# Three projection banks, one chain bank, later transposes and head sums, and weight parts kept in DRAM, in a hybrid decoder trunk

## The chip, the core and the metric

The kernel runs on one core of a Trainium2 chip. Its engines have queues of their own: TensorE (PE, with weight loads as PEld), VectorE (DVE), ScalarE (ACT), GpSimd (POOL) and SyncE (SP), which here only issues DMAs. The accumulator PSUM has eight banks of 128 x 512 float32 numbers. The metric is the device time of one execution in microseconds (us), as the median of several runs.

## What is computed

One layer of a decoder that mixes two kinds of heads, for a prompt of 2048 tokens and, beside it, for eight sequences of four new tokens each (32 sample tokens) with a state from before. The model is 1024 wide; all is float32. Cut to what matters, with the order of the kernel's tiles in mind:

```
h = rmsnorm(x, norm_w)
proj = h @ w_in                               # 1024 -> 3200 columns: 25 tiles of 128
p_rwkv, g_rwkv, u_pool, g_pool = split(proj, [1664, 2176, 2688])
ps = p_rwkv + mu_shift * (previous token's p_rwkv - p_rwkv)
r, k, v, xw, xa = split(ps)                   # 512, 512, 512, 64, 64
decay = exp(-exp(-softplus(-(w0 + tanh(xw) @ w_decay_b)) - 0.5))
a = sigmoid(a0 + xa @ w_aaa_b)
kk = k * k_k;  kk = kk / norm of kk per head;  k = k * (1 + (a - 1) * k_a)
for each token:                               # 8 heads of 64
    sa = S @ (-kk)
    S = S * decay + outer(sa, kk * a) + outer(v, k);  y = S @ r
y = group_norm(y) * gn_w + gn_b
o_rwkv = (y + sum(r * k * r_k) * v) * silu(g_rwkv)
o_pool = (windowed mean of u_pool - u_pool) @ pool_w * pool_scale * silu(g_pool)
out = rmsnorm(x + concat(o_rwkv, o_pool) @ w_out, norm_f)
```

The last rows of the shifted columns and of the pool's input and the last states S are outputs too.

## The kernel before

**Groups and tiles.** The prompt runs in `NG` = 4 groups of 512 tokens. Within a group the 25 column tiles of the projection follow in a fixed order (line 300): tile 12, which holds the two low-rank inputs, and then for each of four pairs of heads j six tiles: r, k, the pool's input, v, the pool's gate and the RWKV gate (`unit`). A projection (`proj`) multiplies a tile of the weights with eight slices `kc` of x. Both factors are split into two parts of the type fp32r, high and low, so there are three matmuls of 128 x 512 for each slice (lines 330 to 332: `xh,wh`, `xl,wh`, `xh,wl`), 24 to a tile, and they gather in one PSUM bank, `pp`. There are two such banks. The bank is read out behind the last matmul by ScalarE and VectorE (`shift`: `t1`, two steps, and `carry`, line 358; `lora_in`: `sa`, line 370; or `gate`). In the last group each tile has two halves of 272 columns, since the sample tokens ride along. The output projection (`out_tile`) comes behind the four groups and uses the same tag.

**The weights.** `w_load` brings a tile of the weights (512 KB, `wr`) by a DMA that ScalarE issues, two tiles ahead. `w_split` makes the parts one tile ahead, when the third slice's matmuls have been written: ScalarE copies `wh` (line 312), and VectorE subtracts to get `wl` (line 313). `wr`, `wh` and `wl` have two buffers each. All this is done anew in each of the four groups: 100 loads and 100 splits.

**The state's recurrence.** It runs for one pair at a time, in chunks of 64 tokens (`NCH` = 8 in a group). `key_norms` squares the keys, splits them (`head_sums`: `h_sq` on ScalarE, line 454, the rest on VectorE), lets `DH` = 6 steps go by and then sums over each head on TensorE (`sq`, line 461; a second such sum is `bo`). `products` makes the matrices within a chunk (`pa`, line 570, from `bk` and `abd`). `solve` has GpSimd solve triangular systems X (lines 636 and 638), which TensorE then transposes (`xt`, line 658). `fold` makes a matrix F for each chunk. `pair_chain` carries the state through the eight chunks: per step two matmuls `ch` (line 751) into one of two `ch` banks; VectorE makes the next state `SV` from partitions 64 to 127 of the bank (line 753), and ScalarE copies the outputs `Y` from partitions 0 to 63 (line 755). At the end `pair_back` norms Y on VectorE (its last step is line 778), waits one step and transposes it on TensorE (`try`, line 788, four matmuls).

**What sets the order.** Each of these is a generator. `proj` yields after each slice's three matmuls, and at each yield `side` lets every lane of the recurrence write its next piece. So a number of yields is a delay in slices of a projection, in the order in which the program is written. A scheduler of the compiler's framework then places the instructions on their engines by priority and by its own model of when each could run, so the order of the program is not kept everywhere. Each engine works through its list in order; an instruction that waits holds up all behind it.

**PSUM.** The eight banks are two each for `pp`, `ch`, `mm` (head sums, `xt`, products and others) and `pt` (`try` among them). The first two projections use the `ch` banks.

Of the kernel before, what the change touches and what calls it, by code (L numbers as in the profile page):

```python
# [9 lines left out]
F32 = mybir.dt.float32  # L10
F32R = mybir.dt.float32r
# [49 lines left out]
def tile_trunk(ctx, tc, xT, xtok, xsT, xstok, par, w_in, wlora, pool_w, w_out, norm_f, st_shift, st_wkv, st_pool,  # L61
# [239 lines left out]
    raws, wts, mark = {}, {}, {}  # L301

    def w_load(i):
        if i < len(order):
            raws[i] = sb.tile([P, KC, P], F32, tag="wr", name=f"wr_{i}")
            nc.scalar.dma_start(raws[i], w_in[order[i][1]])

    def w_split(i):
        if i < len(order):
            hi = sb.tile([P, KC, P], F32R, tag="wh", name=f"wh_{i}")  # L310
            lo = sb.tile([P, KC, P], F32R, tag="wl", name=f"wl_{i}")
            A.activation(hi, raws[i], AF.Copy)  # L312
            V.tensor_tensor(out=lo, in0=raws[i], in1=hi.bitcast(F32), op=sub)  # L313
            wts[i] = hi, lo
            del raws[i]

    def proj(g, m, xs):

        i = order.index((g, m))
        hi, lo = wts.pop(i)  # L320
        w_load(i + 2)
        last = g == NG - 1
        segs = []
        w = 272 if last else 512
        for s in range(2 if last else 1):
            pp = bank("pp" if i >= 2 else "ch", f"pp_{g}_{m}_{s}", 2)
            c = slice(s * w, (s + 1) * w)
            for kc in range(KC):
                xh, xl = xs[kc]
                PE.matmul(pp[:, :w], hi[:, kc, :], xh[:, c], start=(kc == 0), stop=False)  # L330
                PE.matmul(pp[:, :w], hi[:, kc, :], xl[:, c], start=False, stop=False)  # L331
                mark[0] = PE.matmul(pp[:, :w], lo[:, kc, :], xh[:, c], start=False, stop=(kc == KC - 1)).ins  # L332
                if s == 0 and kc == 2:
                    w_split(i + 1)
                if not last or kc % 2:
                    yield
            if g == 0 and m != 12:
                V.tensor_tensor(out=pp, in0=pp, in1=rb0[0], op=mult)
            if last:
                A.activation(spr[:, m, 16 * s:16 * s + 16], pp[:, 256:272], AF.Copy)  # L340
                segs.append((pp, 256 * s, 256))
            else:
                segs.append((pp, 0, G))
        return segs
# [55 lines left out]
    pend = [0]  # L400
    made = [None]
    lanes = {"prod": [], "solve": [], "fold": [], "chain": [], "x": [], "tail": []}
    late = []
# [80 lines left out]
    def key_norms(g, j, u, kk2, prod):  # L484

        nm = f"{g}_{j}"
        a = head_sums(kk2, f"sq_{nm}")
        for _ in range(DH):
            yield
# [220 lines left out]
    def fold(g, j, u):  # L710
# [27 lines left out]
        yield  # L738

    def pair_chain(g, j, u):  # L740
        nm = f"{g}_{j}"
# [3 lines left out]
        for cc in range(NCH):  # L745
            while u["folded"] <= cc:
                yield

            ch = bank("ch", f"ch_{nm}_{cc}", 2, (P, 2, 64))
            for h in range(2):  # L750
# [29 lines left out]
    def pair_back(g, j, u, Y):  # L780
        nm = f"{g}_{j}"
        yn = Y.rearrange("p a h v -> p (a h) v")
        group_norm(yn, yn, P, 8, nm)
        for _ in range(1):
            yield
# [82 lines left out]
    def sample(ret):  # L868
# [154 lines left out]
        for it in range(ST - 1):  # L1023
            yield
            x = bank("ch", f"s_it{it}", 2, (P, 8, 64))
            for hd in range(8):
                PE.matmul(x[0:NS, hd, :], Ab[:, hd, 0, :], sa[:, hd, :], start=True, stop=True)
            V.tensor_tensor(out=sa, in0=x[0:NS], in1=P0, op=add)
            V.tensor_tensor(out=sa, in0=sa, in1=d64, op=mult)
        yield  # L1030
        Y = bank("ch", "s_Y", 2, (P, 8, 64))
        for hd in range(8):
# [87 lines left out]
    def out_tile(o, res, dst, n, wo, nm):  # L1120
# [12 lines left out]
        for f in range(2):  # L1133
            pp = bank("pp", f"po_{nm}_{f}", 2)
            for c in range(8):
# [128 lines left out]
```

## Time and profile before

| | us |
|---|---|
| runs | 1295.18, 1299.73, 1302.32 |
| median | 1299.73 |
| the profiled execution | 1301.06 |
| its span in the trace | 1299.3 |

| engine | busy us | share of the span | instructions |
|---|---|---|---|
| TensorE, matmuls | 1195.8 | 92% | 7229 |
| TensorE, weight loads | 981.2 | 76% | 7229 |
| VectorE | 905.2 | 70% | 2103 |
| ScalarE | 633.3 | 49% | 1438 |
| GpSimd | 532.9 | 41% | 1138 |

HBM gave 100.07 MB and took 20.59 MB in this execution. The four groups lie at about 10 to 266, 266 to 530, 530 to 773 and 773 to 1040 us, the output from 1040 to the end.

How it is read: the span runs from the first to the last event of the trace. Busy times of matmuls and of weight loads overlap. A matmul's row gives its whole passage through the engine (0.39 us for 512 columns), while the next starts 0.23 us after it, so the distances of starts, and not the durations, tell the pace. The granted clock is the share of TensorE's full speed that the chip let it have; 1.00 stands for 2.4 GHz and 0.50 for 1.2 GHz. What stands behind `<-` at an idle time is the instruction that ended the wait, as the profile infers it.

### The profile page before, as it was taken

What the parts mean: (1) busy time and instruction counts of PE and PEld (TensorE: products, weight loads), DVE (VectorE), ACT (ScalarE), POOL (GpSimd) and SP (SyncE); (2) the same over time, 40 slices, a digit from 0 to 9 for tenths busy, and PEclk for the clock granted to TensorE, in tenths of its full rate; (3) what the DMA queues carried; (4) which work ended last, traced back from release to release, by engine and by line L of the source; (5) the groups of instructions that cost most, each with busy time, mean ns of one, the idle gap of its engine ahead of it and who ended that gap; (6) DMA issues with size and microseconds to landing.
All of it is one profiled execution on the core that took longest, in us unless ns stands there. A gap on an engine that the chain in (4) does not pass through costs nothing.

```text
span 1299.3 us, 21202 instructions
## 1 busy us (share of the span) xinstructions
PE 1195.8 (92%) x7229; PEld 981.2 (76%) x7229; DVE 905.2 (70%) x2103; ACT 633.3 (49%) x1438; POOL 532.9 (41%) x1138
## 2 busy tenths in 40 slices
PE   6997999969999898999999998989899999999997
PEld 3775777747777777777777787989898977887685
DVE  6765877776777667866777788666567667744765
ACT  3573545455655454656554557454545453321111
POOL 6064847360728171828083818273517280000000
PEclk7998999988999898999999999999899999998999
DMA  5352433232453332334443334322232444433332
GB/s 182 82 157 62 110 86 92 71 105 79 118 145 102 80 92 80 107 86 136 110 115 95 95 91 122 95 74 87 65 95 68 129 130 140 146 119 98 114 114 72
DMA packets 135371, 134.63 MB, mean 104 GB/s; under 512 B 80480, under 2 KB 97120, under 8 KB 135264
## 3 DMA queue, kind: packets, MB, share of 16 engines
q1 hardware_dynamic: 102432, 78.68, 21.2%
q10 hardware_dynamic: 32832, 54.60, 14.4%
q8 instruction: 57, 0.93, 0.3%
q14 instruction: 50, 0.41, 0.1%
HBM read 100.07 MB, written 20.59 MB: 93 GB/s over the span
## 4 chain that ended last, share of the span: by engine, by line
PE 47%; DVE 14%; ACT 5%; issue 3%; DMA 1%; ACTq 0%; DVEq 0%
PE pp L330 6%; PE pp L331 6%; PE pp L332 5%; PE po_o L1137 5%; PE po_o L1138 4%; PE po_o L1140 4%; PE f L723 3%; PE pa L570 2%; PE ch L751 2%; DVE wl L313 2%; DVE abd L518 1%; PE z L715 1%; PE pb L601 1%; PE q L685 1%; ACT rb L605 1%
## 5 line engine op out<-in xcount | busy, mean ns | idle before, releaser
L330 PE MATMUL pp<-xh,wh 128*128 128x512 f32 (+1 forms) x1000 | 378.7, 380 | 33.8 <-DVE carry L358 8.2
L331 PE MATMUL pp<-xl,wh 128*128 128x512 f32 (+1 forms) x1000 | 373.0, 373 | 5.0 <-DVE xl L256 2.6
L332 PE MATMUL pp<-xh,wl 128*128 128x512 f32 (+1 forms) x1000 | 369.1, 369 | 3.0 <-DVE wl L313 3.0
L330 PEld LDWEIGHTS pp<-xh,wh 128*128 128x128 f32 x1000 | 194.5, 195 | 64.2 <-ACT wh L312 14.7
L636 POOL TENSOR_TENSOR Xt<-X,L 128x60 f32<-128x60 f32 (+24 forms) x496 | 209.0, 421 | 38.9
L331 PEld LDWEIGHTS pp<-xl,wh 128*128 128x128 f32 x1000 | 194.7, 195 | 32.6 <-DVE xl L256 5.1
L332 PEld LDWEIGHTS pp<-xh,wl 128*128 128x128 f32 x1000 | 194.6, 195 | 28.6 <-DVE wl L313 6.2
L638 POOL TENSOR_TENSOR X<-X,Xt 128x60 f32<-128x60 f32 (+24 forms) x496 | 186.4, 376 | 38.9
L313 DVE TENSOR_TENSOR wl<-wr,wh 128x1024 fp32r<-128x1024 f32 x100 | 130.8, 1308 | 35.3 <-ACT wh L312 34.1
L631 POOL TENSOR_TENSOR X<-dmask,a 128x256 f32<-128x256 bf16 x16 | 12.6, 787 | 326.3 <-DVE a L628 326.3
L312 ACT ACTIVATE wh<-wr 128x1024 fp32r<-128x1024 f32 x100 | 105.5, 1055 | 58.1 <-PE pp L331 47.5
L751 PEld LDWEIGHTS ch<-SV,F 128*128 128x128 f32 x512 | 78.4, 191 | 13.4 <-DVE F L726 4.5
L751 PE MATMUL ch<-SV,F 128*128 128x64 f32 x512 | 79.3, 261 | 2.1 <-DVE F L726 1.2
L629 POOL TENSOR_TENSOR L<-L,a 128x1024 f32<-128x1024 f32 x16 | 30.6, 1914 | 123.3 <-DMA L<-dA 123.3
L723 PE MATMUL f<-zbd,ka 128*128 128x256 f32 x256 | 68.4, 388 | 3.5 <-DVE zbd L718 2.1
L1137 PE MATMUL po_o<-woh,oh_o 128*128 128x512 f32 x160 | 67.5, 423 | 1.0 <-ACT woh L1115 1.0
L1138 PE MATMUL po_o<-wol,oh_o 128*128 128x512 f32 x160 | 65.2, 408 | 0.0
L1140 PE MATMUL po_o<-woh,ol_o 128*128 128x512 f32 x160 | 64.5, 403 | 0.0
L755 ACT ACTIVATE Y<-ch 64x128 f32<-64x128 f32 x128 | 34.1, 267 | 55.4 <-DVE SV L753 52.2
L753 DVE TENSOR_TENSOR SV<-ch,lc 64x128 f32<-64x128 f32 x112 | 33.0, 295 | 37.4 <-PE ch L751 34.7
L570 PE MATMUL pa<-bk,abd 128*128 128x192 f32 x256 | 53.1, 347 | 5.7 <-DVE bk L527 3.1
L726 DVE TENSOR_TENSOR F<-f,F 128x512 f32<-128x512 f32 x64 | 44.2, 691 | 19.7 <-PE f L723 18.0
(438 smaller groups left out, 2315.2 us busy)
## 6 DMA issues: line engine op xcount, KB each, us to landing
wr<-in_w_in ACTq DMA_DIRECT2D x100, 512.0 KB
xr<-in_xT SPq DMA_DIRECT2D x32, 256.0 KB
L<-dA SPq DMA_DIRECT2D x64, 128.0 KB
oi<-o_d SPq DMA_DIRECT2D x16, 512.0 KB
xt_g<-in_xtok SPq DMA_DIRECT2D x24, 256.0 KB
F<-ident SPq DMA_DIRECT2D x32, 128.0 KB
rbd<-rd SPq DMA_DIRECT2D x32, 128.0 KB
F<-rd SPq DMA_DIRECT2D x64, 64.0 KB
```

The lines of the kernel that those rows point to most:

```text
L312: A.activation(hi, raws[i], AF.Copy)
L313: V.tensor_tensor(out=lo, in0=raws[i], in1=hi.bitcast(F32), op=sub)
L330: PE.matmul(pp[:, :w], hi[:, kc, :], xh[:, c], start=(kc == 0), stop=False)
L331: PE.matmul(pp[:, :w], hi[:, kc, :], xl[:, c], start=False, stop=False)
L332: mark[0] = PE.matmul(pp[:, :w], lo[:, kc, :], xh[:, c], start=False, stop=(kc == KC - 1)).ins
L636: GP.tensor_tensor(out=tm, in0=X[:, :n, i:i + 1].broadcast_to([P, n, w]), in1=L[:, i + 1:, i].unsqueeze(1).broadcast_to([P, n, w]), op=mult)
L638: done = GP.tensor_tensor(out=X[:, :n, i + 1:], in0=X[:, :n, i + 1:], in1=tm, op=add).ins
L723: PE.matmul(f[:, c].rearrange("p h t -> p (h t)"), u["ka"][:, 2 * b + c, :], zbd[b % 2][:, c].rearrange("p h t -> p (h t)"), start=True, s ...
L751: PE.matmul(ch[:, h, :], fm[cc // 4][:, cc % 4, h, :], sv[cc // 4][:, cc % 4, h, :], start=True, stop=True)
L1137: PE.matmul(pp[:m], hi[:, c, :m], wh, start=(c == 0), stop=False)
L1138: mark[0] = PE.matmul(pp[:m], hi[:, c, :m], wl, start=False, stop=(both and c == 7)).ins
L1140: mark[0] = PE.matmul(pp[:n], lo[:, c, :n], wh, start=False, stop=(c == 7)).ins
```

## The change

**PSUM.** `pp` gets three banks. The chain gets one: `chain_bank` takes it once and uses its two halves in turn (`cc % 2`). The first projection uses this bank, and the second already a `pp` bank; the sample's two tiles take the one bank.

**Delays.** The first head sum `sq` waits for `DH + 2` = 8 yields, `bo` for six as before. `try` waits for five yields in place of one.

**Weights.** There are two DRAM tiles for each tile of the weights (`kept`). In group 0 `w_load` and `w_split` go as before, and SyncE then stores both parts (50 stores of 512 KB). In groups 1 to 3 no tile is split: `w_load` brings both parts from `kept` by two DMAs that ScalarE issues, at the place where the split stood (third slice of the tile before last), into the pairs of buffers of `wh`/`wl` and, for each third tile, of `wr`.

```diff
--- before.py
+++ after.py
@@ -300,17 +300,27 @@
     order = [(g, m) for g in range(NG) for m in [12] + [a + j for j in range(NPAIR) for a in SEQ]]
     raws, wts, mark = {}, {}, {}
 
+
+    kept = [[do.tile([P, KC, P], F32R, tag=f"w{p}_{m}", name=f"w{p}_{m}") for p in "hl"] for m in range(NM)]
+
     def w_load(i):
-        if i < len(order):
+        if i < len(order) and order[i][0]:
+            tags = ("wr", "wr") if i % 3 == 2 else ("wh", "wl")
+            wts[i] = [sb.tile([P, KC, P], F32R, tag=t, name=f"{p}_{i}") for t, p in zip(tags, ("wh", "wl"))]
+            for t, d in zip(wts[i], kept[order[i][1]]):
+                nc.scalar.dma_start(t.bitcast(F32), d.bitcast(F32))
+        elif i < len(order):
             raws[i] = sb.tile([P, KC, P], F32, tag="wr", name=f"wr_{i}")
             nc.scalar.dma_start(raws[i], w_in[order[i][1]])
 
     def w_split(i):
-        if i < len(order):
+        if i in raws:
             hi = sb.tile([P, KC, P], F32R, tag="wh", name=f"wh_{i}")
             lo = sb.tile([P, KC, P], F32R, tag="wl", name=f"wl_{i}")
             A.activation(hi, raws[i], AF.Copy)
             V.tensor_tensor(out=lo, in0=raws[i], in1=hi.bitcast(F32), op=sub)
+            for t, d in zip((hi, lo), kept[order[i][1]]):
+                nc.sync.dma_start(d.bitcast(F32), t.bitcast(F32))
             wts[i] = hi, lo
             del raws[i]
 
@@ -318,12 +328,14 @@
 
         i = order.index((g, m))
         hi, lo = wts.pop(i)
-        w_load(i + 2)
+        late_load = i + 2 < len(order) and order[i + 2][0]
+        if not late_load:
+            w_load(i + 2)
         last = g == NG - 1
         segs = []
         w = 272 if last else 512
         for s in range(2 if last else 1):
-            pp = bank("pp" if i >= 2 else "ch", f"pp_{g}_{m}_{s}", 2)
+            pp = bank("pp", f"pp_{g}_{m}_{s}", 3) if i else bank("ch", "pp_first", 1)
             c = slice(s * w, (s + 1) * w)
             for kc in range(KC):
                 xh, xl = xs[kc]
@@ -332,6 +344,8 @@
                 mark[0] = PE.matmul(pp[:, :w], lo[:, kc, :], xh[:, c], start=False, stop=(kc == KC - 1)).ins
                 if s == 0 and kc == 2:
                     w_split(i + 1)
+                    if late_load:
+                        w_load(i + 2)
                 if not last or kc % 2:
                     yield
             if g == 0 and m != 12:
@@ -399,6 +413,7 @@
     rb0, low = [], []
     pend = [0]
     made = [None]
+    chb = []
     lanes = {"prod": [], "solve": [], "fold": [], "chain": [], "x": [], "tail": []}
     late = []
 
@@ -485,7 +500,7 @@
 
         nm = f"{g}_{j}"
         a = head_sums(kk2, f"sq_{nm}")
-        for _ in range(DH):
+        for _ in range(DH + 2):
             yield
         sq = head_sums_mm(a, f"sq_{nm}")
         sqs = sb.tile([P, 512], F32, tag="tmp", name=f"sqs_{nm}", bufs=3)
@@ -737,6 +752,11 @@
         pend[0] = 0
         yield
 
+    def chain_bank():
+        if not chb:
+            chb.append(bank("ch", "ch", 1, (P, 2, 2, 64)))
+        return chb[0]
+
     def pair_chain(g, j, u):
         nm = f"{g}_{j}"
         fm, sv, lc = u["fm"], u["sv"], u["lc"]
@@ -746,7 +766,7 @@
             while u["folded"] <= cc:
                 yield
 
-            ch = bank("ch", f"ch_{nm}_{cc}", 2, (P, 2, 64))
+            ch = chain_bank()[:, cc % 2]
             for h in range(2):
                 PE.matmul(ch[:, h, :], fm[cc // 4][:, cc % 4, h, :], sv[cc // 4][:, cc % 4, h, :], start=True, stop=True)
             dst = sst[64:128, j] if cc == NCH - 1 else sv[(cc + 1) // 4][64:128, (cc + 1) % 4]
@@ -781,7 +801,7 @@
         nm = f"{g}_{j}"
         yn = Y.rearrange("p a h v -> p (a h) v")
         group_norm(yn, yn, P, 8, nm)
-        for _ in range(1):
+        for _ in range(5):
             yield
         tr = bank("pt", f"try_{nm}", 2)
         for i in range(4):
@@ -1022,13 +1042,13 @@
         V.tensor_tensor(out=sa, in0=P0, in1=d64, op=mult)
         for it in range(ST - 1):
             yield
-            x = bank("ch", f"s_it{it}", 2, (P, 8, 64))
+            x = bank("ch", f"s_it{it}", 1, (P, 8, 64))
             for hd in range(8):
                 PE.matmul(x[0:NS, hd, :], Ab[:, hd, 0, :], sa[:, hd, :], start=True, stop=True)
             V.tensor_tensor(out=sa, in0=x[0:NS], in1=P0, op=add)
             V.tensor_tensor(out=sa, in0=sa, in1=d64, op=mult)
         yield
-        Y = bank("ch", "s_Y", 2, (P, 8, 64))
+        Y = bank("ch", "s_Y", 1, (P, 8, 64))
         for hd in range(8):
             PE.matmul(Y[0:NS, hd, :], p1m[:, hd, 1, :], ident[0:64, 0:64], start=True, stop=False)
             PE.matmul(Y[0:NS, hd, :], Ak[:, hd, 1, :], vt[:, hd, :], start=False, stop=False)
@@ -1131,7 +1151,7 @@
             nc.sync.dma_start(x[f][:n], res[:, f * 512:(f + 1) * 512])
         ss = sb.tile([P, 4, 2], F32, tag="ss", name=f"ss_{nm}")
         for f in range(2):
-            pp = bank("pp", f"po_{nm}_{f}", 2)
+            pp = bank("pp", f"po_{nm}_{f}", 3)
             for c in range(8):
                 wh, wl = wo[c, f]
                 PE.matmul(pp[:m], hi[:, c, :m], wh, start=(c == 0), stop=False)
```

What this does to the engines' order is seen at three places. Numbers behind a name tell apart its buffers.

SyncE, in front of the first projections. `xr_1` and `xr_5` are slices of x, `lw`, `lwx` and `pw` small weights, `F` a constant's fill; before:

```order
L245 DMA xr_7_189<-in_xT 128x512
L163 DMA lw<-in_wlora 128x512
L165 DMA lwx<-in_wlora 128x512
L179 DMA pw<-in_pool_w 128x512
L245 DMA xr_1_175<-in_xT 128x512
L588 DMA F_0_0_524<-ident 64x8x64
```

And after:

```order
L163 DMA lw<-in_wlora 128x512
L165 DMA lwx<-in_wlora 128x512
L323 DMA wh_190<-wh_218 128x1024
L323 DMA wl_191<-wl_219 128x1024
L245 DMA xr_1_227<-in_xT 128x512
L245 DMA xr_5_235<-in_xT 128x512
L179 DMA pw<-in_pool_w 128x512
```

The stores of the first tile's two parts have come to stand between the low-rank weights and `xr_1`.

TensorE, in the projection of k for pair 1 of group 2 (tile 5), where Y of pair 3 of group 1 is transposed (`try_3`); before:

```order
L330 MATMUL pp_5_0_6499<-xh_1_4946,wh_6373 128x512
L331 MATMUL pp_5_0_6499<-xl_1_4947,wh_6373 128x512
L332 MATMUL pp_5_0_6499<-xh_1_4946,wl_6374 128x512
L330 MATMUL pp_5_0_6499<-xh_2_5430,wh_6373 128x512
L788 MATMUL try_3_6434<-ident,Y_3_6069 128x128 [waits DVE_49,PE_49]
L788 MATMUL try_3_6434<-ident,Y_3_6069 128x128 x2
L788 MATMUL try_3_6434<-ident,Y_3_6069 128x128 [waits Activation_49]
L331 MATMUL pp_5_0_6499<-xl_2_5431,wh_6373 128x512
```

And after:

```order
L343 MATMUL pp_5_0_6468<-xl_2_5432,wh_6220 128x512
L344 MATMUL pp_5_0_6468<-xh_2_5431,wl_6221 128x512
L342 MATMUL pp_5_0_6468<-xh_3_5447,wh_6220 128x512
L343 MATMUL pp_5_0_6468<-xl_3_5448,wh_6220 128x512
L808 MATMUL try_3_6448<-ident,Y_3_6054 128x128 [waits DVE_49,PE_49,Activation_49]
L808 MATMUL try_3_6448<-ident,Y_3_6054 128x128 x2
L808 MATMUL try_3_6448<-ident,Y_3_6054 128x128 [waits Activation_49]
L344 MATMUL pp_5_0_6468<-xh_3_5447,wl_6221 128x512
```

The four transposes stood behind the first matmul of slice 2, and stand now behind the second matmul of slice 3: four matmuls later.

TensorE, in the projection of the RWKV gate for pair 0 of group 2 (tile 13), steps 5 and 6 of the chain of pair 3 of group 1 (`po` is the pool's product of pair 0); before:

```order
L330 MATMUL pp_13_0_6195<-xh_4_5470,wh_6119 128x512
L751 MATMUL ch_3_5_6265<-SV_3_1_5409,F_3_1_5534 128x64 [waits DVE_49]
L331 MATMUL pp_13_0_6195<-xl_4_5471,wh_6119 128x512
L751 MATMUL ch_3_5_6265<-SV_3_1_5409,F_3_1_5534 128x64
L332 MATMUL pp_13_0_6195<-xh_4_5470,wl_6120 128x512
L839 MATMUL po_0_6279<-d_0_5966,pw 128x512
L330 MATMUL pp_13_0_6195<-xh_5_5492,wh_6119 128x512
L331 MATMUL pp_13_0_6195<-xl_5_5493,wh_6119 128x512
L332 MATMUL pp_13_0_6195<-xh_5_5492,wl_6120 128x512
L751 MATMUL ch_3_6_6301<-SV_3_1_5409,F_3_1_5534 128x64 [waits DVE_49,Activation_49]
```

And after:

```order
L771 MATMUL ch<-SV_3_1_5411,F_3_1_5533 128x64 [waits Activation_49]
L342 MATMUL pp_13_0_6172<-xh_4_5470,wh_5965 128x512
L771 MATMUL ch<-SV_3_1_5411,F_3_1_5533 128x64
L343 MATMUL pp_13_0_6172<-xl_4_5471,wh_5965 128x512
L344 MATMUL pp_13_0_6172<-xh_4_5470,wl_5966 128x512
L859 MATMUL po_0_6254<-d_0_5953,pw 128x512
L342 MATMUL pp_13_0_6172<-xh_5_5492,wh_5965 128x512
L343 MATMUL pp_13_0_6172<-xl_5_5493,wh_5965 128x512
L344 MATMUL pp_13_0_6172<-xh_5_5492,wl_5966 128x512
L771 MATMUL ch<-SV_3_1_5411,F_3_1_5533 128x64 [waits Activation_49]
```

The matmuls between two steps are the same. The first matmul of a step waited for VectorE, and waits now for ScalarE.

## Rows read from the trace of the kernel before

**Rows 1.** Windows by group: stretch, its us, busy us, clock, DMA share, GB/s.

```profile
0.00:266.00 266.00, 234.82 (x1263) 182.37 (x1264) 186.81 (x385) 138.35 (x290) 136.65 (x295) 0.96 0.37 105
266.00:530.00 264.00, 236.85 (x1349) 189.48 (x1349) 194.50 (x399) 140.06 (x306) 118.37 (x247) 0.95 0.37 101
530.00:773.00 243.00, 229.47 (x1369) 184.94 (x1368) 180.74 (x412) 141.67 (x316) 127.04 (x251) 0.99 0.36 102
773.00:1040.00 267.00, 247.65 (x1959) 233.31 (x1958) 183.00 (x423) 143.23 (x367) 124.64 (x284) 0.97 0.35 94
```

The five busy times with their instructions are TensorE's matmuls, its weight loads, VectorE, ScalarE and GpSimd.

**Rows 2.** Waits of TensorE, 266 to 1040: total us, times, longest.

```profile
PE try L788 <- DVE Y L778: 10.6, 7, 2.5
PE sq L461 <- ACT h_sq L454: 9.4, 4, 3.4
PE pp L330 <- DVE carry L358: 7.7, 5, 4.4
...
PE pp L330 <- ACT sa L370: 3.9, 1, 3.9
PE pp L330 <- DVE st L45: 2.7, 1, 2.7
PE pp L330 <- DVE st L774: 2.6, 1, 2.6
...
PE ch L751 <- DVE SV L753: 0.7, 1, 0.7
```

**Rows 3.** Windows of four stretches at half clock, columns as in rows 1.

```profile
292.30:299.10 6.80, 4.91 (x11) 3.61 (x12) 5.59 (x11) 3.83 (x6) 0.00 (x0) 0.50 0.50 178
...
865.70:869.00 3.30, 3.30 (x17) 3.30 (x16) 3.06 (x12) 0.00 (x0) 2.91 (x7) 0.50 0.39 78
930.60:937.30 6.70, 5.76 (x25) 5.79 (x26) 4.64 (x20) 0.38 (x2) 0.00 (x0) 0.50 0.53 123
1002.30:1009.00 6.70, 6.00 (x26) 6.03 (x27) 6.16 (x23) 0.18 (x2) 0.00 (x0) 0.50 0.28 79
```

**Rows 4.** Timeline of TensorE: start, us, instruction, count, idle before it and releaser.

```profile
608.47 0.39 PE L332 MATMUL pp<-xh,wl 128*128 128x512 f32 x1
608.70 0.39 PE L330 MATMUL pp<-xh,wh 128*128 128x512 f32 x1
611.55 0.63 PE L788 MATMUL try<-ident,Y 128*128 128x128 f32 x4 [2.47 <-DVE Y L778]
...
812.54 0.37 PE L330 MATMUL pp<-xh,wh 128*128 128x272 f32 x1 [2.36 <-DVE carry L358]
...
816.26 0.51 PE L461 MATMUL sq<-h_sq,bonr 128*128 128x512 f32 x1 [0.85 <-ACT h_sq L454]
```

**Rows 5.** Groups by line, 266 to 1040: count, busy us, mean ns, idle before.

```profile
L313 DVE TENSOR_TENSOR wl<-wr,wh 128x1024 fp32r<-128x1024 f32 x74 | 95.7, 1294 | 26.3 <-ACT wh L312 25.5 <-issue 0.3
L312 ACT ACTIVATE wh<-wr 128x1024 fp32r<-128x1024 f32 x74 | 78.1, 1055 | 36.3 <-PE pp L331 32.1 <-DMA wr<-in_w_in 3.7
```

**Rows 6.** Groups by line, whole span: ScalarE's copy of Y.

```profile
L755 ACT ACTIVATE Y<-ch 64x128 f32<-64x128 f32 x128 | 34.1, 267 | 55.4 <-DVE SV L753 52.2 <-DVE sst L753 1.9
```

**Rows 7.** Timeline, all engines: the start, and the first solve's end.

```profile
9.29 0.33 SPq L245 DMA_DIRECT2D xr<-in_xT  x1
9.45 1.04 ACT L312 ACTIVATE wh<-wr 128x1024 fp32r<-128x1024 f32 x1
...
10.53 1.22 DVE L313 TENSOR_TENSOR wl<-wr,wh 128x1024 fp32r<-128x1024 f32 x1 [0.19 <-DMA xr<-in_xT]
...
16.39 1.22 PE L330 MATMUL pp<-xh,wh 128*128 128x512 f32 x2 [2.32 <-ACT xh L255]
...
110.92 1.03 PE L658 MATMUL xt<-ident,X 128*32 128x128 f32 x4 [7.95 <-POOL X L638]
```

**Rows 8.** DMA queues, page part 3: packets, MB, share of 16 engines.

```profile
q1 hardware_dynamic: 102432, 78.68, 21.2%
q10 hardware_dynamic: 32832, 54.60, 14.4%
```

Queue q1 takes SyncE's DMAs, q10 ScalarE's.

## The prediction

> **What bounds the kernel now.** I read the stretches by group of 512 tokens first [rows 1]: in each of the four, TensorE is busy 88 to 94% of the time, VectorE 69 to 74%, ScalarE 52 to 58% and the DMA engines 35 to 37%. TensorE sets the time, and what can be won is what it stands still and what it runs slowly. The waits of TensorE from 266 to 1040 us (groups 1 to 3) say for whom it stands still [rows 2]: all 22 rows of that view add to 58.8 us, and six of the seven shown name a step that the change touches. Four are waits of a projection's first matmul for a PSUM bank that VectorE or ScalarE has not yet read out (`carry`, `sa`, two `st`, in which the last reader sits behind other work on its engine); `try` is the late transpose, `sq` the head sum. The third view is the granted clock behind such a pause [rows 3]: 0.50, the 1.2 GHz level, for 3.3 to 6.7 us, four times after a bank wait. So a pause costs more than itself. The time is the profiled execution's 1301.06 us (span 1299.3), 1.3 us over the median of three, 1299.73.
>
> **Part 1, the third bank.** The bank waits are 3.9 + 2.7 + 2.6 [rows 2], and 4.4 and 2.36 out of the five `carry` waits [rows 2, 4]: 16.0 us. With a third bank the matmul waits for the projection before the one that it waits for now, which was read out a projection earlier. I take the waits as gone, but not all of them as won: behind the pause at 812.54, `sq` at 816.26 still waited 0.85 us for VectorE's keys [rows 4], so those 2.4 us come back there. That leaves **13.6**, between 0 and 16.0. The low-clock stretches behind them hold 4.91 + 3.30 + 5.76 + 6.00 = 20.0 us of TensorE's work [rows 3], which takes half as long at 2.4 GHz: 10.0 at most, **9** taken (the clock can fall for another pause).
>
> **Part 2, the weights' parts.** In groups 1 to 3, 75 tiles are no longer split (74 of them start after 266 us). VectorE loses 74 x 1.294 = 95.7 us, ScalarE 78.1 us [rows 5], or 8.0 us of VectorE in each of 12 pairs. ScalarE issues one DMA more per tile: 0.33 us, by SyncE's issue [rows 7], 75 x 0.33 = 25 us, so it still wins 53. None of this is TensorE's time. It counts where TensorE waits for these engines. `try` does: 10.6 us in seven waits, none over 2.5 [rows 2, 4]. Between the last chain step and the normalised Y two to four tiles are now split, 2.6 us or more of VectorE, so each wait is covered by this alone. It has to be, since the five steps of delay don't hold: the order places `try` of pair 3 in group 1 only four matmuls later (0.23 us each [rows 4]), and in groups 1 and 2 it stands earlier in five of the eight pairs. I take **9.5**, between 4 and 10.6. `sq` waits 9.4 us in four waits [rows 2]; in the order it stays where it was within three matmuls in 12 of the 16 pairs, and the keys' shift that it waits for has little split work behind it. I take **2**, between 0 and 9.4. For all other waits that VectorE and ScalarE cause I take **3**, between 0 and 14. Where VectorE was late, the DMA that brings the weights is late next (the last rival).
>
> What it adds in groups 1 to 3 is 75 x 0.524 = 39.3 MB of reads. The weight queue's 54.60 MB took 14.4% of 1299.3 us [rows 8], 3.43 us of all 16 engines per MB, so 135 us more in 774: the share goes from 0.36 to about 0.53. In group 0 it adds 50 stores, 26.2 MB, 90 us in 266: from 0.37 to 0.71 [rows 1, 8]. Both stay under 1, and a load has more than one and a half tiles (774 / 75 = 10.3 us each) before its first matmul. No row shows a store of this kind, so I bound its harm to others' transfers by 0 and 10 us and take **2**, near zero because no queue fills.
>
> Group 0 pays in two places. At the start the store of the first tile's parts stands in SyncE's queue ahead of the input slice `xr_1`, which is now issued at 9.29. The stores wait for `wh` (9.45 + 1.04) and `wl` (10.53 + 1.22 = 11.75) and take 0.33 us to issue [rows 7], so `xr_1` leaves at about 12.1, 2.8 later, with 1.05 MB ahead of it (3.6 us by the price above). TensorE waits for that slice until 16.39 [rows 7]. Cost between -1 and 6.4 (VectorE's `lwl` steps move into the hole), **3** taken. In the first solve TensorE waits 7.95 us for GpSimd's X at 110.92 [rows 7]; the order brings it there 15 matmuls earlier, so 3.5 us of work that filled the time before now follow the wait, and the loads that GpSimd needs share their engines with stores: **5**, between 1 and 8. Behind SyncE's stores are queued the fills of F, `rbd` and L; each stands behind a tile that is split earlier than they are ready, so I cost that at nothing beyond the 2 above.
>
> **Part 3, one bank for the chain.** The next chain step's matmul waited for VectorE's SV (0.7 us in all [rows 2]); now the order has it wait for ScalarE's Y, which itself waits for SV (52.2 us idle [rows 6]). Each of 7 x 16 = 112 links gets 0.267 us longer [rows 6]: 29.9 us if TensorE waits for each, 0.7 if the order covers them as it covers SV today. The matmuls between two steps stand as before, and the order was made with the wait in it, so I take **4**, near the lower end.
>
> The Trainium skill, "PSUM — Partial Sum Buffer", section "Summary: rules for kernel authors", wants a matmul to target a different bank from the one that is being read. By that rule the sum would carry the full 29.9. [rows 6] shows that reads in this bank are already made to wait for one another, although VectorE reads partitions 64 to 127 and ScalarE 0 to 63, which the same page, in the section on bank collisions, allows at the same time; no run here shows them together.
>
> The Trainium skill, "DMA: Bandwidth & Descriptors", section "Anatomy of one DMA", fits a transfer as 2.0 us plus its bytes at 436 GB/s (for GpSimd's DMAs). By that an estimate for a pair of parts is 4.4 us, inside the lead of a tile and a half; no row here gives a landing time.
>
> **Sum.** 13.6 + 9 + 9.5 + 2 + 3 = 37.1 won; 2 + 3 + 5 + 4 = 14 paid. 1301.1 - 23.1 = 1278; against the median, about **1277 us**.
>
> **Rivals.**
> 1. The waits move on. If the chain on VectorE and ScalarE ends last everywhere, as at 816.26, the third bank and the clock behind it win nothing: 1301.1 - 14.5 + 14 = 1301. For it: `sq` stood right behind one of the five. Against: behind the waits of 4.4 and 2.7 no such row.
> 2. Everything that waits on VectorE and ScalarE falls. The 58.8 us and the 10.0 of clock go, the costs are half of mine and a little shift remains: 1301.1 - 68.8 + 9 = 1241. For it: 96 us less on VectorE. Against: `sq`, and slices of x that wait for DMAs.
> 3. The chain's single bank decides: 29.9 in place of 4, 1278 + 26 = 1304. For it: 52.2 us of ScalarE's waiting inside the chain [rows 6]. Against: matmuls of the projection fill the steps.
> 4. Slower: weights come late. The first matmul of each projection in groups 1 to 3 waits for a pair of loads that ScalarE issues in its own order, behind waits of its own. From 23 / 75 = 0.31 us a tile the gain is gone; at 0.5 us it is 1278 + 38 = 1316. For it: two issues, twice the bytes, and more stores and loads in turn. Against: today ScalarE's split idles 3.7 us for weights in 74 tiles [rows 5], 0.05 each.
>
> That the change doesn't do what it says is partly so (`try`, `sq` hardly move in the order), and is in the sum.
>
> **How the numbers follow.** Forecast 0.57, rival 1 0.08, rival 2 0.17, rival 3 0.07, rival 4 0.11. A run can tell about 0.5% from no change: 1293.2 to 1306.2. Of the forecast 0.03 lies inside that band, and 0.01 of rival 3 above it. Faster 0.57 + 0.17 - 0.03 = 0.71; same 0.08 + 0.06 + 0.03 = 0.17; slower 0.11 + 0.01 = 0.12. The range must leave out at most 0.2: rival 4 (0.11) and the lower half of rival 2 (0.085) go, so 1242 to 1305; the unknown costs (37.1 won could be 17 to 60, 14 paid 1 to 54) lie mostly in it.
>
> **What would show it.** Right: in groups 1 to 3 no wait of a projection's first matmul on `carry`, `sa` or `st` above 1 us; `try` under 2 us in all; VectorE's busy time down by about 96 us and ScalarE's by 78; chain matmuls waiting for Y under 8 us; `xr_1`'s issue at about 12 us; DMA share near 0.7 in group 0 and 0.5 after. Wrong: `sq` or chain waits that grow by what the banks gave; a first matmul that waits for a weight DMA; group 0 longer than 280 us; low-clock stretches as many as now.

## The result, and the profile after

The changed kernel takes **1286.22 us** (median of six runs, 1283.79 to 1289.64); the kernel before, beside it, 1301.61 (1295.18 to 1307.32). The ratio is **0.9873**, 95% interval 0.9839 to 0.9907. The forecast was 1277, the range 1242 to 1305. The profiled execution took 1285.28 us, its span 1283.6. The ratios here and below are the record's, of fast runs alone (two of e1's twelve are slow, 1305.89 and 1308.84 us, and count in its median only), so they are not quite the quotients of the medians.

Windows of the changed kernel, cut where the first projection of a group begins, with the columns of [rows 1]; the last is the output:

```profile
0.00:285.50 285.50, 243.16 (x1266) 187.89 (x1266) 191.24 (x387) 141.31 (x295) 126.94 (x295) 0.92 0.59 193
285.50:525.30 239.80, 229.63 (x1345) 185.68 (x1346) 159.74 (x371) 112.14 (x273) 114.44 (x244) 0.99 0.53 164
525.30:767.30 242.00, 230.51 (x1367) 187.96 (x1366) 158.73 (x388) 118.10 (x291) 113.19 (x254) 0.98 0.54 157
767.30:1026.50 259.20, 243.43 (x1962) 230.71 (x1961) 157.09 (x399) 122.15 (x344) 123.93 (x288) 0.98 0.47 141
1026.50:1283.60 257.10, 246.31 (x1294) 190.42 (x1293) 160.55 (x487) 70.00 (x162) 25.41 (x60) 0.97 0.38 121
```

The same cuts in the kernel before lie at 270.3 and 1040.3:

```profile
0.00:270.30 270.30, 235.26 (x1265) 182.56 (x1265) 190.31 (x389) 142.54 (x299) 140.40 (x302) 0.95 0.36 104
270.30:1040.30 770.00, 713.82 (x4671) 607.84 (x4672) 554.78 (x1230) 421.06 (x978) 366.52 (x775) 0.97 0.36 99
1040.30:1299.30 259.00, 246.71 (x1295) 190.82 (x1293) 160.14 (x486) 69.72 (x163) 25.93 (x63) 0.97 0.36 116
```

Groups 1 to 3 went from 770.0 us to 741.0, so they won 29.0. Group 0 went from 270.3 to 285.5 and lost 15.2. The output won 1.9. TensorE stood idle in groups 1 to 3 for 770.0 - 713.8 = 56.2 us before and 37.4 after. The granted clock was 0.50 there for 45.8 us before and 27.3 after; half of TensorE's busy time in these stretches, 19.8 and 12.5 us, is what the lower level cost. Group 0 gave this back: it was at 0.50 for 25.8 us before and 47.8 after, at a cost of 8.5 and 15.8 us, and TensorE's idle time in it rose from 35.0 to 42.3. So of its 15.2 us 7.3 are idle time and 7.3 clock, and over the whole span the lower level cost 35.1 us in either profile.

The waits of TensorE in groups 1 to 3 of the changed kernel answer to [rows 2]:

```profile
PE try L808 <- DVE Y L798: 12.8, 11, 3.2
PE pa L585 <- DVE bk L542: 9.0, 3, 3.3
PE sq L476 <- ACT h_sq L469: 4.9, 2, 3.4
PE pp L342 <- ACT xh L204: 4.5, 2, 2.4
PE pa L585 <- DVE nwt_g L55: 1.8, 1, 1.8
...
PE ch L771 <- ACT Y L775: 0.8, 3, 0.5
PE pp L342 <- DVE carry L372: 0.5, 1, 0.5
```

All rows of this view add to 39.1 us, before to 58.8 between the same cuts. The waits for a bank are gone but for 0.5 us, the chain waits 0.8 us for ScalarE's Y; `try` has not fallen, and the products `pa` are new near the top. The DMA queues, against [rows 8], show the stores in q1 and the doubled loads in q10:

```profile
q1 hardware_dynamic: 109632, 104.90, 26.7%
q10 hardware_dynamic: 43632, 93.93, 23.2%
```

Much of group 0's loss is made at the start. SyncE's and TensorE's timelines there, against [rows 7]:

```profile
10.57 0.33 SPq L323 DMA_DIRECT2D wh<-wh  x1
11.83 0.33 SPq L323 DMA_DIRECT2D wl<-wl  x1
12.21 1.23 SPq L245 DMA_DIRECT2D xr<-in_xT  x2
```

```profile
20.76 0.80 PE L342 MATMUL pp_first<-xh,wh 128*128 128x512 f32 x1 [6.64 <-ACT xh L255]
...
26.09 0.80 PE L343 MATMUL pp_first<-xl,wh 128*128 128x512 f32 x1 [2.46 <-DVE xl L256]
...
32.95 0.50 PE L343 MATMUL pp_first<-xl,wh 128*128 128x512 f32 x1 [1.57 <-DVE xl L256]
...
34.32 0.63 PE L344 MATMUL pp_first<-xh,wl 128*128 128x512 f32 x1
...
42.01 0.40 PE L342 MATMUL pp<-xh,wh 128*128 128x512 f32 x1
```

The last two lines are the 25th and the 49th matmul of the projections. The same two before:

```profile
25.03 0.40 PE L332 MATMUL pp<-xh,wl 128*128 128x512 f32 x1
...
35.98 0.39 PE L330 MATMUL pp<-xh,wh 128*128 128x512 f32 x1
```

`xr_1` leaves at 12.21, behind the two stores. TensorE goes on at 20.76 in place of 16.39, waits for VectorE's `xl` at 26.09 and 32.95 (before it waited 1.66 us at 27.55), and runs at half clock until 30.2 us in place of 22.6. The scheduler mixes the first two tiles, of 24 matmuls each, so the delay is read by counting: the 25th matmul comes at 34.3 and was at 25.0, and the 49th, with as many behind it as two tiles have, comes at 42.0 and was at 36.0. In a second profile of the changed kernel (e11) it comes at 43.1. So the start lost 6 to 7 us that last.

### The profile page after: what moved, and what is told of

It is laid out like the page before. It is cut to its first block, busy times and chain, and to the rows that moved or that the text cites. A ratio compares the mean times of both kernels' runs of the same rounds, so it can differ in the third digit from the quotient of the medians.

```text
span 1283.6 us, 21090 instructions
## 1 busy us (share of the span) xinstructions
PE 1193.0 (93%) x7229; PEld 982.6 (77%) x7229; DVE 827.3 (64%) x2028; ACT 563.7 (44%) x1363; POOL 503.9 (39%) x1138
## 5 line engine op out<-in xcount | busy, mean ns | idle before, releaser
L342 PE MATMUL pp<-xh,wh 128*128 128x512 f32 (+1 forms) x992 | 367.6, 371 | 7.5 <-ACT xh L204 4.5
L343 PE MATMUL pp<-xl,wh 128*128 128x512 f32 (+1 forms) x992 | 364.7, 368 | 1.4 <-DVE xl L205 1.4
L344 PE MATMUL pp<-xh,wl 128*128 128x512 f32 (+1 forms) x992 | 363.1, 366 | 0.2 <-DVE wl L321 0.2
L342 PEld LDWEIGHTS pp<-xh,wh 128*128 128x128 f32 x992 | 189.9, 192 | 33.7 <-ACT xh L204 5.6
L343 PEld LDWEIGHTS pp<-xl,wh 128*128 128x128 f32 x992 | 189.8, 191 | 25.3 <-DVE xl L205 2.7
L344 PEld LDWEIGHTS pp<-xh,wl 128*128 128x128 f32 x992 | 189.5, 191 | 23.6 <-DVE wl L321 1.7
L651 POOL TENSOR_TENSOR Xt<-X,L 128x60 f32<-128x60 f32 (+24 forms) x496 | 191.9, 387 | 38.8
L653 POOL TENSOR_TENSOR X<-X,Xt 128x60 f32<-128x60 f32 (+24 forms) x496 | 179.8, 363 | 38.9
L771 PEld LDWEIGHTS ch<-SV,F 128*128 128x128 f32 x512 | 75.2, 191 | 19.7 <-ACT Y L775 8.7
L585 PE MATMUL pa<-bk,abd 128*128 128x192 f32 x256 | 56.2, 366 | 11.0 <-DVE bk L542 9.0
L733 DVE COPY zbd<-z 64x256 f32<-64x256 f32 x64 | 27.2, 427 | 55.8 <-ACT zbd L732 54.6
L775 ACT ACTIVATE Y<-ch 64x128 f32<-64x128 f32 x128 | 34.3, 268 | 64.3 <-DVE SV L773 56.3
L585 PEld LDWEIGHTS pa<-bk,abd 128*128 128x128 f32 x256 | 49.7, 217 | 15.8 <-DVE bk L542 7.0
```

The lines of the kernel that those rows point to most:

```text
L585: PE.matmul(pa[:, c, :], abd[:, 2 * b + c, :], bk[:, 2 * b + c, :], start=True, stop=True)
L651: GP.tensor_tensor(out=tm, in0=X[:, :n, i:i + 1].broadcast_to([P, n, w]), in1=L[:, i + 1:, i].unsqueeze(1).broadcast_to([P, n, w]), op=mult)
L653: done = GP.tensor_tensor(out=X[:, :n, i + 1:], in0=X[:, :n, i + 1:], in1=tm, op=add).ins
L771: PE.matmul(ch[:, h, :], fm[cc // 4][:, cc % 4, h, :], sv[cc // 4][:, cc % 4, h, :], start=True, stop=True)
```

## The experiments

Each ratio is against the kernel before, run beside it on the same chip; the stretches come from one profiled execution each, cut as above. Two profiles of the changed kernel differ by 2.6 us at most in any one group; in another order of the instructions a few us more can move between groups.

| kernel | median us | ratio, 95% interval | group 0 | groups 1 to 3 | of them idle | output |
|---|---|---|---|---|---|---|
| before | 1301.61 | 1 | 270.3 | 770.0 | 56.2 | 259.0 |
| changed | 1286.22 | 0.9873, 0.9839 to 0.9907 | 285.5 | 741.0 | 37.4 | 257.1 |
| e1 banks alone | 1298.57 | 0.9966, 0.9929 to 1.0003 | 274.0 | 764.9 | 48.6 | 259.6 |
| e2 weights alone | 1291.85 | 0.9925, 0.9893 to 0.9956 | 279.5 | 760.7 | 53.0 | 255.5 |
| e3 delays alone | 1306.80 | 1.0047, 1.0023 to 1.0071 | 274.0 | 768.6 | 54.3 | 259.5 |
| e4 first store late | 1278.28 | 0.9819, 0.9781 to 0.9858 | 276.1 | 743.9 | 37.9 | 255.6 |
| e5 = e4, no delays | 1278.06 | 0.9817, 0.9771 to 0.9862 | 269.6 | 746.5 | 41.6 | 261.7 |
| e6 = e4, `wl` only | 1292.99 | 0.9935, 0.9907 to 0.9963 | 273.1 | 759.9 | 46.8 | 262.8 |
| e7 chain bank alone | 1302.16 | 0.9997, 0.9970 to 1.0024 | 269.3 | 768.2 | 51.3 | 258.8 |
| e8 = e4, `try` at ten | 1282.37 | 0.9838, 0.9793 to 0.9883 | 273.3 | 746.2 | 42.2 | 264.0 |
| e9 = e4, VectorE's work back | 1293.94 | 0.9952, 0.9923 to 0.9980 | 281.7 | 753.8 | 41.0 | 255.7 |
| e10 = e4, ScalarE's work back | 1294.81 | 0.9943, 0.9917 to 0.9968 | 277.1 | 754.6 | 45.7 | 262.6 |
| e11 changed, again | 1284.91 | 0.9873, 0.9844 to 0.9901 | 286.3 | 741.9 | 37.8 | 254.4 |
| e12 e4, again | 1277.39 | 0.9834, 0.9805 to 0.9864 | 275.4 | 745.9 | 37.3 | 254.1 |

### Each part alone (e1, e2, e3)

e1 takes the changed kernel's lines on `bank` and `chain_bank` into the kernel before; e2 those on `kept`, `w_load` and `w_split`; e3 only

```diff
-        for _ in range(DH):
+        for _ in range(DH + 2):
...
-        for _ in range(1):
+        for _ in range(5):
```

> The kernel before with the banks' part alone: three banks for the projections, one for the chain; weights and delays as before. In the two profiles, groups 1 to 3 went from 770.0 us (270.3 to 1040.3) to 741.0 (285.5 to 1026.5), group 0 from 270.3 to 285.5. Theory A (the terms add up as in the prediction): the waits of a projection's first matmul for `carry`, `sa` and `st`, 16 us, go, and the half clock behind them; the chain pays 4. Groups 1 to 3 at about 752 us, group 0 at 270 as before, ratio about 0.986. Rival B (the gain is the splits' that VectorE and ScalarE no longer make): without the weights' part the chain on VectorE and ScalarE still ends last, the waits come back at `sq`, `pa` and `try`; groups 1 to 3 above 765, ratio 0.996 to 1.003.

> The kernel before with the weights' part alone: parts stored in group 0 and loaded in groups 1 to 3; two banks for the projections, two for the chain, delays as before. Theory A: only what waits on VectorE's queue falls, at most 12 us of 770 in groups 1 to 3 (758 or more), the bank waits for `sa` and `st` stay or shrink by half, and group 0 pays 10 to 15 us (280 to 285): ratio 0.998 to 1.004. Rival B: groups 1 to 3 fall by 25 or more, to under 745, ratio about 0.99. For group 0 alone: if the stores make its loss of 15 us in the changed kernel, it is 280 or more here; if the new order of the work does, it is 270 to 275 here and 280 or more with the banks alone.

> The kernel before with the two delays alone: the head sum `sq` after eight yields, the transpose `try` after five. Theory A: the scheduler does not keep the delays, so the waits for `try` (10.6 us from 266 to 1040 before) stay at 7 us or more and the time within 0.4% of before: ratio 0.996 to 1.004. Rival: the delays do cover VectorE's norm; `try` under 3 us in all, ratio 0.992 or less.

With the banks alone the waits of TensorE in groups 1 to 3 begin with

```profile
PE try L794 <- DVE Y L784: 17.6, 9, 4.4
PE sq L462 <- ACT h_sq L455: 13.1, 6, 3.2
```

No row of this view names a bank (before: 16.9 us, the four rows of [rows 2]). But `try` and `sq` rose from 20.0 us [rows 2] to 30.7. Rival B held, at the edge of its bound (764.9 us): most of what the third bank frees is waited for two steps later. With the weights alone it is the other way round:

```profile
PE try L801 <- DVE Y L791: 7.6, 7, 2.0
PE pp L341 <- DVE carry L371: 5.2, 3, 2.3
...
PE pp L341 <- ACT t L366: 4.1, 1, 4.1
PE pp L341 <- DVE nwt L55: 3.8, 1, 3.8
...
PE pp L341 <- DVE rps L369: 3.2, 1, 3.2
...
PE pp L341 <- DVE kps L369: 2.8, 2, 1.4
```

`try` falls, `sq` is at 1.9 us in two small rows, and the waits for a bank stay: 19.1 us in the five rows on `pp`. Theory A's 758 us or more for groups 1 to 3 held (760.7); its ratio, 0.998 to 1.004, did not, and 0.9925 is nearer to Rival B's. Group 0 took 279.5 us here and 274.0 with the banks alone, so the stores, by the place of the first one (below), make most of the loss.

In these profiles the parts alone won 5.1 and 9.3 us in groups 1 to 3, and together, with the delays, 29.0; without the delays (e5) 23.5. It looks as if each part removed the wait that the other's gain would otherwise run into. The medians don't show that. The profiled executions of e1 and e2 took 1300.28 and 1297.78 us, 1.7 and 5.9 above their medians, and e1's twelve runs have a mean granted clock of 0.969, the profiled one 0.964. By the ratios e1 won 0.34% and e2 0.75%, about 14 us, and e2 paid for the first store what e4 and e12 win back below, 7.5 to 7.9 us. Together these make about 22 us; e5, which has both parts and not this loss, won 1.83%, 24 us, with an interval of 18 to 30. That the parts win more together than alone stays open.

The delays alone were slower by 0.5%, just beyond what A expected, and `try` waited 12.6 us for Y. They do not even move it: in this trace as many projection matmuls stand between the chain's last step and `try` as before in 13 of the 14 pairs whose `try` lies among projections. In e2, which has no new delays, there are 2 to 26 fewer in 11 of the 14. Why e3 is slower stays open.

### The start (e4, e11, e12)

```diff
-            for t, d in zip((hi, lo), kept[order[i][1]]):
-                nc.sync.dma_start(d.bitcast(F32), t.bitcast(F32))
+            held.append((hi, lo, order[i][1]))
+            while i and held:
+                *parts, m = held.pop(0)
+                for t, d in zip(parts, kept[m]):
+                    nc.sync.dma_start(d.bitcast(F32), t.bitcast(F32))
```

> The changed kernel, but the stores of the first tile's two parts are written one tile later, so that the input slice `xr_1` stands ahead of them in SyncE's queue; all else as changed. Theory A (the start's loss is that slice's): `xr_1` leaves at about 9.3 us in place of 12.2, the second tile's first matmul comes at about 25 to 28 us in place of 34.3 (25.0 before), the half clock there ends earlier, and the 7 to 9 us stay won to the end: ratio about 0.981 against before, 1277 us. Rival: the time comes back within group 0 (the first solve on GpSimd ends no earlier, since its start is set by the inputs and the decay): group 1 begins at 283 or later as in the changed kernel, 1285 us.

SyncE's queue and TensorE's first wait in this kernel:

```profile
9.43 0.33 SPq L245 DMA_DIRECT2D xr<-in_xT  x1
10.68 0.33 SPq L326 DMA_DIRECT2D wh<-wh  x1
```

```profile
14.88 0.80 PE L345 MATMUL pp_first<-xh,wh 128*128 128x512 f32 x1 [0.65 <-ACT xh L255]
```

Theory A held: the 25th matmul, which the expectation calls the second tile's first, comes at 23.6 us and the 49th at 33.7, and the time stays won to the end. Since the intervals overlap, both were run again beside each other.

> The changed kernel once more, beside the one with the late first store on the same chip, since their ratios against before (0.9873, 0.9819) have intervals that overlap. Theory A (the late first store wins 8 us): 0.986 to 0.989 here, 0.980 to 0.984 in its neighbour. Rival (the difference was the chip's): both within 0.25% of each other. Its profile is a second execution of the same order: group 0 at 283 to 287 us, groups 1 to 3 at 737 to 745.

> The kernel with the late first store once more, beside the changed kernel on the same chip. Theory A: 0.980 to 0.984 against before and 0.3% or more under the changed kernel; group 0 at 274 to 278 us. Rival: within 0.25% of the changed kernel.

Theory A held: 1284.91 and 1277.39 us. The first gap was 7.9 us, this one 7.5; group 0 took 286.3 and 275.4. Writing the first store one tile later makes the kernel that beats both.

### The delays and the chain's bank (e5, e8, e7)

e5 is e4 with six yields and one yield again, e8 is e4 with `range(10)` for `try`; e7 has the change's `chain_bank` lines in the kernel before, with two `pp` banks.

> The kernel with the late first store, but with both delays as before (six yields for `sq`, one for `try`). Alone, the delays made the kernel before slower (ratio 1.0047). Theory A: they do nothing of use here either, since the waits for `try` were 12.8 us with them and 10.6 before; ratio against before 0.978 to 0.985, as with the late first store (0.9819), `try` within 4 us of 11.2. Rival: with the bank waits gone the delays are what keeps `sq` and `try` from taking their place (with the banks alone and no delays, `sq` rose to 14.8 and `try` to 18.9 us): here `sq` and `try` together rise by 8 us or more and the ratio is 0.988 or more.

> The kernel with the late first store, and `try` after ten yields in place of five. Theory A (the scheduler places `try` where its own model has Y ready, whatever the delay): `try` stays at 8 us or more, ratio 0.979 to 0.985 as with five yields (0.9819). Rival (the delay was only too short): `try` under 4 us, ratio 0.976 or less.

> The kernel before with one bank for the chain and still two for the projections (one bank stays unused); weights and delays as before. Theory A (the chain's links are covered by the projections' matmuls): waits of `ch` for Y under 3 us, ratio 0.998 to 1.004. Rival (each of 112 links gets 0.27 us longer): 20 us or more, ratio 1.015 or more.

e5 is as fast as e4 (Theory A); `try` and `sq` together wait 16.0 us there and 15.3 in e4. Its group 0, 269.6 us, is as short as before, with all stores in it. In e8 the order did give way, and the time did not. Its waits in groups 1 to 3:

```profile
PE pa L588 <- DVE bk L545: 7.2, 4, 3.1
PE sq L479 <- ACT h_sq L472: 6.7, 2, 4.2
...
PE try L811 <- DVE Y L801: 3.8, 6, 1.6
PE pa L588 <- DVE ka L590: 3.8, 2, 2.8
```

`try` fell from 11.2 to 3.8 us as the rival said, but TensorE's idle time in groups 1 to 3 went from 37.9 to 42.2. What `try` no longer waits, TensorE waits elsewhere: all waits in groups 1 to 3 add to 43.6 us, in e4 to 39.5, with `sq` and `pa` at 20.4 in place of 17.6, and projections and `z` at 14.9 in place of 8.1. In e7 the chain waits for ScalarE's Y

```profile
PE ch L757 <- ACT Y L761: 1.0, 4, 0.3
```

and the ratio is 0.9997: Theory A. The estimate of 29.9 us is excluded by this run; reads and matmuls do take turns in this bank, but the projections' matmuls fill the gaps. The prediction had set that estimate beside the Trainium skill's rule to target another bank than the one that is read ("PSUM — Partial Sum Buffer", section "Summary: rules for kernel authors"); here the price of not doing so is these 1.0 us of waits.

### Whose work (e6, e9, e10)

e6 keeps `wl` alone in DRAM. e9 and e10 put one engine's time back in e4, at the old place of the split:

```diff
+                    if g and i + 1 < len(order):
+                        for n in (3, 3, 2):
+                            V.tensor_tensor(out=dummy[:, :n], in0=idents[:, :n], in1=idents[:, :n], op=sub)
```

(e10: `A.activation(dummy[:, :n], idents[:, :n], AF.Copy)`).

> The kernel with the late first store, but only the low part `wl` is kept in DRAM; in groups 1 to 3 ScalarE makes `wh` from the loaded tile again (78 us of ScalarE), VectorE subtracts nothing. Theory A (it is VectorE's 96 us that hold the banks' gain): groups 1 to 3 at 740 to 750 us as with both parts kept, ratio 0.981 to 0.988. Rival (ScalarE's share matters as much, since it reads out `t1`, `sa` and copies Y): groups 1 to 3 at 755 or more, with new waits of projections for ScalarE (`wh`, `t1`), ratio 0.992 or more.

> The kernel with the late first store (both parts kept), with VectorE's work put back and nothing else: for each tile of groups 1 to 3, at the place of the old split, three VectorE subtractions on a constant, together as long as a 128x1024 one (about 1.3 us, 96 us in all); their result is used nowhere. Theory A (VectorE's 96 us hold most of the gain that the two parts make only together): groups 1 to 3 back to 758 us or more (743.9 with the late first store), ratio 0.990 or more. Rival (ScalarE's 78 us hold it): groups 1 to 3 under 750, ratio 0.986 or less, and the loss appears in the sister kernel with ScalarE's work instead.

> The same with ScalarE's work put back: three copies of a constant per tile, together as long as a 128x1024 one (about 1.1 us, 78 us in all). Theory A (VectorE holds the gain): groups 1 to 3 under 750 us, ratio 0.986 or less. Rival (ScalarE does): groups 1 to 3 at 758 or more, ratio 0.990 or more, with new waits of projections for what ScalarE reads out (`t1`, `sa`) and of `sq` for `h_sq`.

What was put back, as groups by line of e9 and of e10, is more than meant, 119 and 107 us in place of 96 and 78:

```profile
L356 DVE TENSOR_TENSOR dummy<-ident 128x384 f32<-128x384 f32 (+1 forms) x222 | 119.0, 536 | 3.4
```

```profile
L356 ACT ACTIVATE dummy<-ident 128x384 f32<-128x384 f32 (+1 forms) x222 | 107.3, 483 | 16.1 <-DMA dS<-sqs 10.3 <-DVE wl L323 1.5 <-issue 0.9
```

No theory held whole. Each ratio is where it should be if this engine's work counts, 0.990 or more, but both kernels lost only some 10 us in groups 1 to 3 (753.8 and 754.6 against 743.9, with 758 or more expected), while the medians are about 16 us above e4's in either. In e6, with VectorE free and ScalarE copying `wh`, groups 1 to 3 took 759.9, as its rival said; 3.9 us of that are waits for the DMA of `wl`, which it loads only one tile ahead. So the gain of the weights' part is not VectorE's alone. How much of it is whose can't be said more closely, since each kernel also has an order of its own (e9's group 0, in which nothing was put back, is 5.6 us longer than e4's). One cause was not tested by itself: in the kernel before, ScalarE's copy `wh` waited for TensorE, 32.1 us [rows 5], and held up what stood behind it on ScalarE. The copies put back in e10 have no such wait.

## Why the prediction came out as it did

The sum, term by term, against the two profiles (us; minus is won):

| term | forecast | measured |
|---|---|---|
| bank waits | -13.6 | 16.9 to 0.5: -16.4 |
| clock behind them, groups 1 to 3 | -9 | 19.8 to 12.5: -7.3 |
| `try` for Y | -9.5 | 10.6 to 12.8: +2.2 |
| `sq` | -2 | 9.4 to 4.9: -4.5 |
| other waits, the chain's among them | -3 + 4 | 21.9 to 20.9: -1.0 |
| start, by the 49th matmul | +3 | +6.0 |
| rest of group 0 (first solve, stores) | +5 + 2 | +9.2 |
| output | 0 | -1.9 |
| all | -23.1 | -15.8 |

The waits sum to -19.7 and the clock to -7.3; groups 1 to 3 fell by 29.0, so 2.0 us there lie in neither. That the sum came within 7.4 us is in part luck: `try` missed by 11.7 us and group 0 by 5.2, while the bank waits, `sq`, the output and what lies in no term gave 9.2 back. The range, 63 us wide, would have held no change too. Of the prediction's signs of being wrong, one came: group 0 is longer than 280 us. Two rows were read a little off, which moves no term: the longest stretch of [rows 3] is 6.80 us, and the row at 816.26 [rows 4] names ScalarE's `h_sq`, not VectorE's keys.

**Right: direction, size within the range, and the mechanism of the banks.** The waits for `carry`, `sa` and `st` are gone, and in groups 1 to 3 half clock fell with them, from 45.8 to 27.3 us. Alone, though, the banks' part comes near rival 1: by the sum's terms e1 was to have a ratio of 0.986, and it has 0.9966, with no wait for a bank left and 10.7 us more at `try` and `sq`. The sum took the 13.6 us as if hardly anything would wait in their place.

**Wrong: `try`.** The step said that each wait was covered by two to four splits that fall away. But the scheduler places `try` by its own model, and with the splits gone it places it earlier: in five of eight pairs here, as the order had shown, and in 11 of 14 in e2. There are now 11 waits of it in place of 7. The weights' part alone brought them from 10.6 to 7.6 us (e2), the banks' part alone to 17.6 (e1), both without delays to 14.2 (e5). It has also taken a bank's place ahead of a low clock [rows 3]: in its wait of 3.21 us for Y the clock falls to the 1.2 GHz level.

```profile
997.28 1.11 PE L808 MATMUL try<-ident,Y 128*128 128x128 f32 x4 [3.21 <-DVE Y L798]
```

```profile
996.10:1003.00 6.90, 5.72 (x23) 5.72 (x23) 4.58 (x9) 1.21 (x4) 0.57 (x1) 0.51 0.12 43
```

**Mis-sized: the start.** The mechanism was right (`xr_1` at "about 12.1", measured 12.21), the price was not: 6.0 us by the 49th matmul and 7.1 in e11, twice the 3 taken and about the upper bound of 6.4 (by the 25th it is 9.3). The bound counted the slice's own delay, 4.4 us as it came out. It left out that with the longer pause the clock stays at half until 7.6 us later (in e11 until 38.8 us), and that VectorE's `xl` comes late too: TensorE's waits for it in group 0's start went from 2.6 to 4.0 us. The sum has no term for the clock in group 0, and there it cost 7.3 us more.

**Half right: the rest of group 0.** Its 9.2 us are near the 7 forecast, for another reason. The wait for the first X is 7.6 us, before 7.95 [rows 7]; the stores harm nothing that shows, since e5 has them all and its group 0 takes 269.6 us. What remains goes with the order: e4 and e12, which differ from e5 in the delays alone, have 276.1 and 275.4.

**Right: the chain's bank and the loads.** The chain's price of 4 us was too careful (0.8 us of waits). In groups 1 to 3 no matmul of a projection waits for a DMA of weights (one weight load does, for 0.2 us): rival 4 had no row. The DMA share was forecast at 0.71 in group 0 and 0.53 behind it; it was 0.59, and 0.47 to 0.54. VectorE's busy time fell by 905.2 - 827.3 = 77.9 us and not by 96, ScalarE's by 69.6 and not 78; the splits did go (`wl` and `wh` from 100 steps to 25 each). Added step by step, VectorE's time fell by 87.0 us, since its other steps took 13 us longer, and ScalarE's by 78.0; the busy time counts stretches in which steps overlap once.

## What to carry to other kernels

Where an engine waits for a chain that runs over two others, the waits are not terms that add: take one away and a later step waits instead (in e1 16.9 us of waits for a bank went and 10.7 came up at `try` and `sq`; in e8 `try` lost 7.4 us of waits and all waits together rose by 4.1). Before pricing a removed wait in full, ask which row would wait next. Whether two parts help each other has to be read from medians: one profiled execution lay 5.9 us from its median here, as much as was to be told apart. A store put into a queue ahead of the first loads costs more than its own delay (`xr_1` left 2.8 us later, and the kernel lost 7.5 to 7.9); write it behind what the start needs.

## What the runs showed of the hardware

One VectorE step, `abd`, takes 0.75 us in the median of 32 and up to 3.12. A long one, here in group 3 of the changed kernel, runs while GpSimd multiplies its masks:

```profile
L533 DVE SCALAR_TENSOR_TENSOR abd<-kps,pr,lam x32: 731/752/3117, 59.1 to 988.9; 64x512 f32<-64x512 f32 x32
```

```profile
800.23 1.29 POOL L663 TENSOR_TENSOR F<-F,mkr 64x512 f32<-64x512 f32 x1
...
800.30 3.01 DVE L533 SCALAR_TENSOR_TENSOR abd<-kps,pr,lam 64x512 f32<-64x512 f32 x1
```

```profile
807.07 1.68 PE L585 MATMUL pa<-bk,abd 128*128 128x192 f32 x8 [3.34 <-DVE bk L542]
```

TensorE then waits 3.34 us for `bk`, which stands behind `abd` on VectorE. The Trainium skill, "SBUF — State Buffer", section "Who interferes with whom", says that a VectorE instruction with two SBUF inputs and a GpSimd instruction that reads SBUF exclude each other; the trace agrees, with 3.01 us beside GpSimd's work where the median is 0.75. No run here moved the masks, so it is not shown that they make the step long.

The output, whose code is the same in all kernels but for a third bank, took 254.1 to 264.0 us by the profiles, with 10 to 28 us of it at half clock. Why some orders fall to the lower level more often there stays open. Two executions of one kernel differ as well: in groups 1 to 3 the lower level cost 13.0 us in e4 and 17.4 in e12. So the clock can hide or feign some 5 us in any comparison of single profiles.
